# The forward substitution of eight head pairs: VectorE or POOL, in a hybrid decoder step whose order a planner sets

## The chip, the core and the metric

The kernel runs on one core of one Trainium2 chip. Its engines are TensorE (PE; its weight loads are listed as PEld), VectorE (DVE), ScalarE (ACT), GpSimd (POOL) and SyncE (SP, which here issues DMAs). The metric is the device time of one launch in microseconds; lower is better.

## What is computed

One step of a decoder layer, for 512 prompt tokens and 8 sample tokens together (520 columns, in chunks of 260), width 1024: an RMS norm, then two branches on the same normalised input, dilated window attention (three groups of 8 heads) and RWKV-7 time mixing (16 heads of 64), merged by sigmoid gates, an output projection and a SwiGLU FFN. What the change touches is the time mixing, whose reference is a scan over tokens:

```python
def step(S, inp):
    r_t, w_t, k_t, v_t, kk_t, a_t = inp
    sa = jnp.einsum('bhij,bhj->bhi', S, -kk_t)
    S = (S * w_t[:, :, None, :] + sa[..., None] * (kk_t * a_t)[:, :, None, :]
         + v_t[..., None] * k_t[:, :, None, :])
    return S, jnp.einsum('bhij,bhj->bhi', S, r_t)
...
y_a = o_a @ lw['w_proj_a']
y_b = o_b @ lw['w_proj_b']
merged = jax.nn.sigmoid(gate_a) * y_a + jax.nn.sigmoid(gate_b) * y_b
out = merged @ lw['w_out']
```

## The kernel before

**Large products.** Every weight is split into two parts (`whi`, `wlo`) and every activation too (`hh`, `hl`), and each 128x128 block takes three matmuls of 128x260 (written `mm<-hh,whi` and so on). They carry most of the program. ACT makes `whi`, DVE makes `wlo`, from blocks that SP loads.

**Time mixing in chunks.** The 16 heads are 8 pairs, p = 0 to 7, and the 512 prompt tokens are 8 chunks of 64. For each pair there are these steps:

- `pair(p)` prepares the operands: matrices `GH` (two tiles, one for each head), `AR`, `KB`, `VT`, and starts `back(p)`, which is the rest.
- `solve(p)` inverts the diagonal 32x32 blocks of the lower triangular matrices in `GH` by forward substitution. Four DMAs on SP bring the blocks to DRAM (`TD`), four bring the coefficients back with one block a partition (`LT`, 128 partitions). `X` starts as the identity by five memsets. Then come 31 steps of two operations: `xt = X[:, :m, s] * LT[s]` and `X += xt`, with m = s // 4 + 1 and w = 31 - s, so m·w elements a partition (1 to 76; the sum over the steps is 1560). Four DMAs write `X` to DRAM (`TE`), four read it back into `GH`. Transposes on DVE (`T`) and small matmuls (`ax<-T,GH`, `ax<-GH,QI`) finish the 64x64 inverse. `SOLVERS` = 2 solves may be in flight (two buffers each of `LT` and `X`), and every `SOLVE` = 3 steps the code hands over to the planner.
- `turn_a(p)` and the first part of `chain(p)` multiply by the inverse. The sequence of `ax<-T,GH` and what follows up to the first chain step is called the turn here. It needs pair p-1's turn to be past.
- `chain(p)` walks the eight chunks: PE `ch<-VTr,GH` and `ch<-AR`, then ACT writes `GH`, then PE `ch<-GH,KB`, then DVE updates the state in `AR`. The steps of one pair are serial; two pairs' chains can run side by side. After them come the output products (`ch<-GH`, `ch<-AR`, called the y product), a copy, a group norm, and the pair's output `OB`.

**What sets the order.** One build-time planner, `Weave`, writes the whole program. It keeps a model clock for each engine (`Clocks`), in which each operation has a price (`Unit.price`), and takes in turn from a main list of large products and from side generators (`pair`, `back`, the sample tokens) whatever its model says is ready. So the engine on which an operation stands, and its price there, move other engines' instructions. The model's prices of the two engines:

```python
if self.name == "POOL":
    return 0.25 + n / 480
if self.name != "PE":
    return 0.07 + n / 960
```

The main list is: the attention and r, k, v projections; 16 gate jobs (`fill`) and 8 jobs of w_proj_a (`pas`), which fill the space between chains; then w_proj_b, w_out, FFN. The w_proj_a jobs load `ga` on POOL's queue into buffers that share the tag `LT`, multiply on DVE and store to `TAD` on POOL's queue. w_proj_b's output blocks n = 0 and n = 1 are begun with the first 7 of 8 input blocks, which need `OB` of pairs 0 to 6 alone, and closed with the last one.

Every operation is recorded by one helper, so all rows show line L380; rows are told apart by tile names.

Of the kernel before, what the change touches and what calls it, by code (L numbers as in the profile page):

```python
# [12 lines left out]
ALU = mybir.AluOpType  # L13
# [12 lines left out]
NP = HB // 2  # L26
# [195 lines left out]
def _bc(ap, shape):  # L222
    return ap.to_broadcast(shape)
# [242 lines left out]
def program(tc, I, O):  # L466
    nc = tc.nc
    ck = Clocks()
    V, S, G, SY = (Unit(n, e, tc, ck) for n, e in (("DVE", nc.vector), ("ACT", nc.scalar), ("POOL", nc.gpsimd), ("SP", nc.sync)))
# [4 lines left out]
    wv = Weave(ck, tc)  # L474
    uid = [0]

    def nm(s):
        uid[0] += 1
        return f"{s}_{uid[0]}"

    def pool(name, stack, **kw):
        return Pool(stack.enter_context(tc.tile_pool(name=name, bufs=1, reuse_waits="tile", **kw)), ck)
# [13 lines left out]
    def bank():  # L496
        return axp.tile([128, 512], FP, name=nm("ax"), tag="ax", bufs=3)
# [153 lines left out]
    def full(tag, bufs=1, dt=FP):  # L651
        return ep.tile([128, NT], dt, name=nm(tag), tag=tag, bufs=bufs)
# [621 lines left out]

    def solve(p):
        r2, QI, GH = rw["r2"], rw["QI"], rw["GH", p]
        TD = drp.tile([4, NC, 32, 32], FP, name=nm("TD"))
        TE = drp.tile([4, NC, 32, 32], FP, name=nm("TE"))
        for q in range(4):
            b = q % 2  # L1280
            SY.dma_start(out=TD[q].rearrange("c s t -> s c t"), in_=GH[q // 2][q * 32:q * 32 + 32, :, b * 32:b * 32 + 32])
        if p >= SOLVERS:
            yield from wv.until("x", p - SOLVERS)

        LT = r2.tile([128, 31, 32], FP, name=nm("LT"), tag="LT", bufs=SOLVERS)
        Xs = r2.tile([128, 8, 32], FP, name=nm("X"), tag="X", bufs=SOLVERS)
        V.memset(Xs[:], 0.0)
        for a in range(4):
            V.memset(Xs[a * 32:a * 32 + 32].rearrange("p m t -> p (m t)")[:, a:256:36], 1.0)
        yield (TD,)  # L1290
        for a in range(4):
            SY.dma_start(out=LT[a * 32:a * 32 + 32], in_=TD[:, :, :31].rearrange("q c s t -> (q c) s t"))
        yield (LT,)
        for s in range(31):
            m = s // 4 + 1
            w = 31 - s
            t = r2.tile([128, 128], FP, name=nm("xt"), tag="xt")
            tv = t[:, :m * w].rearrange("p (m w) -> p m w", m=m)
            V.tensor_tensor(out=tv, in0=_bc(Xs[:, :m, s:s + 1], [128, m, w]),
                            in1=_bc(LT[:, s:s + 1, s + 1:], [128, m, w]), op=ALU.mult)  # L1300
            V.tensor_tensor(out=Xs[:, :m, s + 1:], in0=Xs[:, :m, s + 1:], in1=tv, op=ALU.add)
            if s % SOLVE == SOLVE - 1:
                yield (Xs,)
        yield (Xs,)
        te = TE[:].rearrange("q c (j b) t -> (q c) j b t", b=4)
        for a in range(4):
            SY.dma_start(out=te[:, :, a], in_=Xs[a * 32:a * 32 + 32])
        wv.set("x", p)
        yield (TE,)
        for q in range(4):  # L1310
            b = q % 2
            SY.dma_start(out=GH[q // 2][q * 32:q * 32 + 32, :, b * 32:b * 32 + 32], in_=TE[q].rearrange("c j t -> j c t"))
        yield GH
        if p:
            yield from wv.until("at", p - 1)
        T1 = r2.tile([128, NC, 32], FP, name=nm("T1"), tag="AT")
        for h in range(2):
            V.transpose(out=T1[H[h]], in_=GH[h][H[h], :, 0:32])
        yield T1, BANK
        ps = bank()  # L1320
        for c in range(NC):
            for h in range(2):
                a, b = (slice(h * 64 + i, h * 64 + i + 32) for i in (0, 32))
                E.matmul(ps[b, c * 32:c * 32 + 32], lhsT=GH[h][a, c, 32:64], rhs=T1[a, c], start=True, stop=True)
        for h in range(2):
            b = slice(h * 64 + 32, h * 64 + 64)
            S.copy(out=QI[b], in_=ps[b, :256].rearrange("p (c x) -> p c x", c=NC))
        yield QI, BANK
        ps = bank()
        for c in range(NC):  # L1330
            for h in range(2):
                a, b = (slice(h * 64 + i, h * 64 + i + 32) for i in (0, 32))
                E.matmul(ps[a, c * 32:c * 32 + 32], lhsT=QI[b, c], rhs=GH[h][b, c, 32:64], start=True, stop=True)
        for h in range(2):
            a = slice(h * 64, h * 64 + 32)
            S.copy(out=GH[h][a, :, 32:64], in_=ps[a, :256].rearrange("p (c x) -> p c x", c=NC))
        wv.set("solved", p)
        yield GH
# [128 lines left out]
    def back(p):  # L1467
        yield from solve(p)
        yield from wv.until("w0", p)
        yield from turn_a(p)  # L1470
        yield from chain(p)
        if p == NP - 3:
            for i in range(NP - 2):
                yield from wv.until("pair", NP - 1)
                t = full("tmp", 2)
                G.dma_start(out=t[:, :T], in_=OBD[:, i])
                yield (t,)
                o = ob_tile(i)
                split(o[:, 0, :T], o[:, 1, :T], t[:, :T])
                wv.set("ob", i)  # L1480
# [208 lines left out]
    def pb_pre(n):  # L1689
        def pre():  # L1690
            if n == 0:
                yield from wv.until("ob", NP - 3)
                hctx.close()
                mp = mrg["pool"] = pool("mg", mctx, side="right")
                mrg["h"] = mp.tile([128, KD, NT], FR, name="mh")
                mrg["l"] = mp.tile([128, KD, NT], FR, name="ml")
            gb = gp_.tile([128, NT], FP, name=nm("gb"), tag="g", bufs=2)
            ta = full("tmp", 2)
            G.dma_start(out=gb[:], in_=GD[:, KD + n])
            G.dma_start(out=ta[:], in_=TAD[:, n])  # L1700
            mrg[n] = gb, ta
            yield ()
        return pre
# [264 lines left out]
```

## Time and profile before

| | us |
|---|---|
| median of 3 runs | 1312.92 (1310.77 to 1315.44) |
| profiled execution | 1316.53 |
| its span, first to last instruction | 1314.8 |
| PE busy | 1264.7 (96%) |
| DVE busy | 843.7 (64%) |
| ACT busy | 610.6 (46%) |
| POOL busy | 175.0 (13%) |
| mean granted TensorE clock | 0.983 |

Of the page, the lines of slices give an engine's busy share in 40 equal parts of the span, here 32.9 us each, in tenths. The groups give busy time and mean duration of instructions with the same tiles. A row of the timeline begins with start and duration in us, and ends with what the engine waited for, if it did. `windows` rows give busy time in a stretch.

### The profile page before, as it was taken

Reading aid. Unit: us, or ns where it says so; the run is one execution under the profiler, and the core shown is the slowest. Engines: PE = TensorE matmul, PEld = TensorE weight load, DVE = VectorE, ACT = ScalarE, POOL = GpSimd, SP = SyncE. Lnnn points to the kernel's source line nnn. Section 1 sums busy time; section 2 is a strip of 40 time slices with the busy share of each in tenths; the row PEclk is TensorE's granted clock in tenths of the full one; section 3 lists DMA queues with packets and bytes.
Section 4 is the critical chain, followed back from the end, with each engine's and each line's share of the span. In section 5 each row is a group of like instructions: output and inputs, shape, how many; then the busy total and the mean of one; then the engine's idle time right before and its main releaser. Section 6 shows DMA issues by size and latency. Waiting matters only on the chain.

```text
span 1314.8 us, 29468 instructions
## 1 busy us (share of the span) xinstructions
PE 1264.7 (96%) x11738; PEld 1197.5 (91%) x11738; DVE 843.7 (64%) x2221; ACT 610.6 (46%) x1554; POOL 175.0 (13%) x261
## 2 busy tenths in 40 slices
PE   7999999999989989999999999999999999999996
PEld 7998999989978878888888888999999999999996
DVE  6956866954869998886986665555843444332333
ACT  5244244366656656675785665334433232222220
POOL 1300100100223332121123122110200000000000
PEclk9999999999989999997999999999999999999998
DMA  6523654634245554543245454552222222223331
GB/s 215 158 94 96 213 178 146 221 112 172 69 131 136 152 147 141 143 156 97 77 139 168 123 175 157 182 192 85 81 97 97 97 89 89 97 93 89 89 101 65
DMA packets 92137, 169.48 MB, mean 129 GB/s; under 512 B 42416, under 2 KB 47568, under 8 KB 92000
## 3 DMA queue, kind: packets, MB, share of 16 engines
q1 hardware_dynamic: 60880, 102.46, 24.6%
q0 software_dynamic: 14512, 46.47, 11.5%
q10 hardware_dynamic: 16608, 18.68, 4.3%
q8 instruction: 92, 1.51, 0.5%
q14 instruction: 45, 0.37, 0.1%
HBM read 133.20 MB, written 27.94 MB: 123 GB/s over the span
## 4 chain that ended last, share of the span: by engine, by line
PE 64%; DVE 15%; issue 9%; DMA 6%; ACT 4%; POOL 1%; SPq 1%; ACTq 0%; DVEq 0%; POOLq 0%
PE mm L380 51%; PE ax L380 8%; PE ch L380 5%; DVE wlo L380 2%; DVE X L380 1%; DVE xt L380 1%; DMA fb<-FD 1%; DMA sw<-raw 1%; ACT KB L380 1%; DVE k L380 1%; DMA raw<-w_in 1%; SPq L380 1%; DVE raw L380 1%; DVE qk L380 1%; DVE GH L380 1%
## 5 line engine op out<-in xcount | busy, mean ns | idle before, releaser
L380 PE MATMUL mm<-hh,whi 128*128 128x260 f32 x1136 | 340.2, 299 | 0.8 <-ACT gt L380 0.8
L380 PE MATMUL mm<-hh,wlo 128*128 128x260 f32 x1136 | 325.4, 286 | 4.3 <-DVE wlo L380 4.3
L380 PE MATMUL mm<-hl,whi 128*128 128x260 f32 x1136 | 325.7, 287 | 0.0
L380 ACT CAST whi<-raw 128x1024 fp32r<-128x1024 f32 (+1 forms) x165 | 170.1, 1032 | 324.4 <-PE mm L380 290.6
L380 DVE TENSOR_TENSOR wlo<-raw,whi 128x1024 fp32r<-128x1024 f32 (+1 forms) x165 | 197.9, 1199 | 140.2 <-ACT whi L380 137.0
L380 PEld LDWEIGHTS mm<-hh,whi 128*128 128x128 f32 x1136 | 215.7, 190 | 13.3 <-issue 6.0
L380 PEld LDWEIGHTS mm<-hh,wlo 128*128 128x128 f32 x1136 | 215.4, 190 | 6.5 <-DVE wlo L380 5.8
L380 PEld LDWEIGHTS mm<-hl,whi 128*128 128x128 f32 x1136 | 215.5, 190 | 1.4 <-issue 0.2
L380 PE MATMUL mm<-h2l,whi 128*128 128x260 f32 x608 | 171.5, 282 | 0.0
L380 PE MATMUL mm<-h2h,wlo 128*128 128x260 f32 x608 | 171.4, 282 | 0.0
L380 PE MATMUL mm<-h2h,whi 128*128 128x260 f32 x608 | 171.4, 282 | 0.0
L380 PEld LDWEIGHTS mm<-h2h,wlo 128*128 128x128 f32 x608 | 114.5, 188 | 0.0
L380 PEld LDWEIGHTS mm<-h2l,whi 128*128 128x128 f32 x608 | 114.4, 188 | 0.0
L380 PEld LDWEIGHTS mm<-h2h,whi 128*128 128x128 f32 x608 | 114.4, 188 | 0.0
L380 PE MATMUL mm<-fh,wlo 128*128 128x260 f32 x388 | 109.6, 282 | 0.0
L380 PE MATMUL mm<-fh,whi 128*128 128x260 f32 x388 | 109.5, 282 | 0.0
L380 PE MATMUL mm<-fl,whi 128*128 128x260 f32 x388 | 109.5, 282 | 0.0
L380 PEld LDWEIGHTS mm<-fh,whi 128*128 128x128 f32 x388 | 73.1, 188 | 0.0
L380 PEld LDWEIGHTS mm<-fl,whi 128*128 128x128 f32 x388 | 73.0, 188 | 0.0
L380 PEld LDWEIGHTS mm<-fh,wlo 128*128 128x128 f32 x388 | 72.9, 188 | 0.0
L380 DVE TENSOR_TENSOR xt<-X,LT 128x60 f32<-128x60 f32 (+24 forms) x248 | 60.3, 243 | 3.6
L380 DVE TENSOR_TENSOR X<-X,xt 128x60 f32<-128x60 f32 (+24 forms) x248 | 57.6, 232 | 3.8
(390 smaller groups left out, 2588.8 us busy)
## 6 DMA issues: line engine op xcount, KB each, us to landing
raw<-w_in SPq DMA_DIRECT2D x77, 512.0 KB, 3.7
raw<-w_gate SPq DMA_DIRECT2D x22, 512.0 KB, 3.2
raw<-w_up SPq DMA_DIRECT2D x22, 512.0 KB, 3.2
raw<-w_down SPq DMA_DIRECT2D x16, 512.0 KB, 3.5
kt<-kcache POOLq DMA_DIRECT2D x24, 256.0 KB, 3.7
kt<-vcache POOLq DMA_DIRECT2D x24, 256.0 KB, 3.5
sw<-raw ACTq DMA_DIRECT2D x64, 65.0 KB, 3.6
GD<-gt ACTq DMA_DIRECT2D x16, 260.0 KB, 3.0
```

What stands on the lines that cost most here:

```text
L380: r = f(*a, **k)
```

## The change

The forward substitution's memsets and its 62 operations a pair are issued on POOL (`G`) instead of DVE (`V`). The main list gains one wait: block n = 1 of w_proj_b may not begin until the last pair's chain has recorded its output copy.

```diff
     def solve(p):
         r2, QI, GH = rw["r2"], rw["QI"], rw["GH", p]
+        B = G
...
-        V.memset(Xs[:], 0.0)
+        B.memset(Xs[:], 0.0)
         for a in range(4):
-            V.memset(Xs[a * 32:a * 32 + 32].rearrange("p m t -> p (m t)")[:, a:256:36], 1.0)
+            B.memset(Xs[a * 32:a * 32 + 32].rearrange("p m t -> p (m t)")[:, a:256:36], 1.0)
...
-            V.tensor_tensor(out=tv, in0=_bc(Xs[:, :m, s:s + 1], [128, m, w]),
+            B.tensor_tensor(out=tv, in0=_bc(Xs[:, :m, s:s + 1], [128, m, w]),
                             in1=_bc(LT[:, s:s + 1, s + 1:], [128, m, w]), op=ALU.mult)
-            V.tensor_tensor(out=Xs[:, :m, s + 1:], in0=Xs[:, :m, s + 1:], in1=tv, op=ALU.add)
+            B.tensor_tensor(out=Xs[:, :m, s + 1:], in0=Xs[:, :m, s + 1:], in1=tv, op=ALU.add)
...
     def pb_pre(n):
...
+            if n == 1:
+
+                yield from wv.until("chain", NP - 1)
```

The order of PE's instructions changes with it, since the planner prices these operations differently. The numbers behind tile names count the tiles as they are made, and are those of one program alone. PE in before, where the chain of pair 4 (`VTr_7889`) runs beside that of pair 5 (`VTr_8320`), with gate work (`mm`) between:

```order
L380 MATMUL ch_10211<-VTr_7889,GH_7440 64x64
L380 MATMUL ch_10211<-VTr_7889,GH_7441 64x64
L380 MATMUL ch_10211<-AR_7327 64x64 x2
L380 MATMUL ch_10218<-VTr_8320,GH_8126 64x64
L380 MATMUL ch_10218<-VTr_8320,GH_8127 64x64
L380 MATMUL ch_10218<-AR_7936 64x64 x2
L380 MATMUL mm_10175<-hh,whi_9889 128x260
L380 MATMUL mm_10175<-hl,whi_9889 128x260
L380 MATMUL mm_10175<-hh,wlo_9890 128x260
L380 MATMUL mm_10175<-hh,whi_9889 128x260
L380 MATMUL mm_10175<-hl,whi_9889 128x260
L380 MATMUL mm_10175<-hh,wlo_9890 128x260
```

PE in after, in the chain of pair 5 (`VTr_8417`):

```order
L380 MATMUL ch_10663<-VTr_8417,GH_8007 64x64
L380 MATMUL ch_10663<-VTr_8417,GH_8008 64x64
L380 MATMUL ch_10663<-AR_7843 64x64 x2
L380 MATMUL ch_10663<-GH_8007,KB_8400 64x64
L380 MATMUL ch_10663<-GH_8008,KB_8400 64x64
L380 MATMUL ch_10705<-VTr_8417,GH_8007 64x64
L380 MATMUL ch_10705<-VTr_8417,GH_8008 64x64
L380 MATMUL ch_10705<-AR_7843 64x64 x2
L380 MATMUL ch_10705<-GH_8007,KB_8400 64x64
L380 MATMUL ch_10705<-GH_8008,KB_8400 64x64
```

In before a chain step is followed by another pair's step and by gate matmuls; in after the same pair's next step follows at once. Over the whole of PE, 3366 matmuls of 128x260 stand ahead of pair 4's turn in before and 3786 in after; from that turn to the last chain's end it is 540 and 258. The total is the same.

POOL in before, at the sample tokens' work for the first pair:

```order
L380 TENSOR_TENSOR st_4602<-st_4602,sg_4289 128x512
L380 TENSOR_TENSOR svd_4865<-uk,sel 48x256
L380 TENSOR_TENSOR svd_4876<-uk,sel 48x256
L380 DMA oo_5097<-OTD 128x512
L380 DMA OAD<-oac_4632 128x512
```

POOL in after, at the same place:

```order
L380 TENSOR_TENSOR st_4602<-st_4602,sg_4289 128x512
L380 TENSOR_TENSOR xt_4805<-X_4617,LT_4616 128x31
L380 TENSOR_TENSOR X_4617<-X_4617,xt_4805 128x31
L380 TENSOR_TENSOR xt_4808<-X_4617,LT_4616 128x30
L380 TENSOR_TENSOR X_4617<-X_4617,xt_4808 128x30
```

Fifty operations of the first solve now stand between the state update (`st`) and the sample tokens' `svd`. At the end of the solves, in after, the operations of the last one stand behind the transfers of w_proj_a:

```order
L380 DMA ga_10770<-GD 128x520
L380 DMA TAD<-ga_10770 128x520
L380 DMA br_11077<-GTD 128x512
L380 DMA ga_10841<-GD 128x520
L380 DMA OBD<-KB_8400 128x512
L380 DMA bvr_11496<-BVD 128x512
L380 DMA TAD<-ga_10841 128x520
L380 TENSOR_TENSOR xt_11079<-X_10211,LT_10210 128x60
L380 TENSOR_TENSOR X_10211<-X_10211,xt_11079 128x6x10
```

So the last solve's operations, and its hold on one of the two `LT` buffers, last until the transfers of w_proj_a ahead of them on POOL's queue have been issued.

## The prediction

> **What bounds the kernel now.** I read the busy times and slices first, then the chain that ended last, then windows cut at the solves and the chains, and last the timeline of single rows.
>
> ```profile
> span 1314.8 us, 29468 instructions
> PE 1264.7 (96%) x11738; PEld 1197.5 (91%) x11738; DVE 843.7 (64%) x2221; ACT 610.6 (46%) x1554; POOL 175.0 (13%) x261
> DVE  6956866954869998886986665555843444332333
> POOL 1300100100223332121123122110200000000000
> PE 64%; DVE 15%; issue 9%; DMA 6%; ACT 4%; POOL 1%; SPq 1%; ACTq 0%; DVEq 0%; POOLq 0%
> ```
>
> PE is busy for 96% of the span: whatever shortens another engine can win only what PE idles, and whatever makes PE idle costs in full. POOL is nearly empty and DVE is full in slices 12 to 16 (361 to 526 us), which speaks for moving work. The next fence has the three stretches in which the eight pairs are solved and chained (the third begins at pair 4's turn and ends at pair 7's y product), and then solve work alone on DVE in the same stretches (us, DVE busy). The columns of the first three rows are us, then busy PE, PEld, DVE, ACT, POOL with counts, then granted clock, DMA share, GB/s.
>
> ```profile
> 365.00:468.00 103.00, 95.02 (x864) 88.10 (x863) 92.13 (x268) 59.22 (x145) 32.19 (x44) 0.97 0.48 134
> 468.00:672.00 204.00, 195.01 (x2189) 171.99 (x2188) 171.58 (x595) 134.90 (x421) 48.22 (x68) 0.95 0.44 130
> 672.10:810.70 138.60, 132.56 (x1694) 116.18 (x1694) 94.39 (x342) 92.86 (x307) 30.13 (x50) 0.99 0.49 152
> ...
> sum 445.60, DVE 120.79; mean DVE 40.26
> ```
>
> Ahead of pair 4's turn PE idles 8.0 + 9.0 = 17.0 us, and the clock's shortfall (3% of 95.0, 5% of 195.0) is another 12.6 us. That 30 us is all that a freer DVE could return there. What PE waited for in 365 to 672 us (us, times, longest):
>
> ```profile
> PE mm L380 <- DVE wlo L380: 3.3, 4, 1.4
> PE ax L380 <- DVE sd L380: 3.2, 1, 3.2
> PE ax L380 <- DVE sg L380: 2.7, 1, 2.7
> PE ch L380 <- DVE AR L380: 1.6, 2, 1.4
> ```
>
> **The moved arithmetic.** A solve is 31 steps of two TENSOR_TENSORs, 62 in all, over 2 x 1560 = 3120 elements per partition (the sum of m·w in the code). On DVE all of them cost 60.3 + 57.6 = 117.9 us, with 40 memsets beside them. POOL never ran this operation on these tiles; its nearest rows are two of its own TENSOR_TENSORs, of 256 and of 512 elements:
>
> ```profile
> L380 DVE TENSOR_TENSOR xt<-X,LT 128x60 f32<-128x60 f32 (+24 forms) x248 | 60.3, 243 | 3.6
> L380 DVE TENSOR_TENSOR X<-X,xt 128x60 f32<-128x60 f32 (+24 forms) x248 | 57.6, 232 | 3.8
> L380 DVE MEMSET X<- x40: 65/65/272, 334.8 to 696.0; 32x8 f32 x32, 128x256 f32 x8
> L380 POOL MEMSET kw<- 128x32 f32 x1 | 0.1, 118 | 0.0
> 621.20 0.61 POOL L380 TENSOR_TENSOR svd<-uk,sel 48x256 f32<-48x256 f32 x1 [10.61 <-ACT uk L380]
> 645.54 1.04 POOL L380 TENSOR_TENSOR st<-st,sg 128x512 f32<-128x512 f32 x1 [8.43 <-PE ax L380]
> ```
>
> The line through the two POOL rows is (1.04 - 0.61)/256 = 1.68 ns an element and 0.18 us fixed. A solve is then 62 x 0.18 + 3120 x 1.68 ns = 16.4 us, 0.26 us an operation against DVE's 0.24. From below the price is POOL's small memset, 0.118 us; from above the whole 0.61 us of the svd row. I take 0.26, because these operations have 1 to 76 elements and so lie below both rows, plus an estimated 0.06 of hand-over (DVE's rows below leave 0.04 between dependent operations): 0.32 us, 20 us a solve, 160 us for eight. The five memsets cost some 5 x 0.118 us a solve and lie beside the load of the coefficients, so nothing. The four stores and loads around a solve stay on SP's queue, now behind POOL's last step instead of DVE's; weight loads queued behind them are two jobs ahead of PE. I take nothing for that, with a bound of 10 us for all (1.3 a pair).
>
> Is POOL then the bound? In the three windows it is busy 32.2 + 48.2 + 30.1 = 110.5 us of 445.6. With 8 x 16.4 = 131 more it has 242. It is not, at this price.
>
> There is a contention to see:
>
> ```profile
> 517.30 0.61 POOL L380 TENSOR_TENSOR svd<-uk,sel 48x256 f32<-48x256 f32 x1 [2.27 <-ACT uk L380]
> 517.33 0.61 DVE L380 TENSOR_TENSOR xt<-X,LT 128x24 f32<-128x24 f32 x1
> 517.98 0.18 DVE L380 TENSOR_TENSOR X<-X,xt 128x24 f32<-128x24 f32 x1
> 518.20 0.18 DVE L380 TENSOR_TENSOR xt<-X,LT 128x16 f32<-128x16 f32 x1
> ```
>
> A DVE row with two operands that starts 0.03 us after a POOL row ends with it, at 0.61 us instead of about 0.18. So POOL's 496 operations can hold up DVE, and DVE's long ones POOL's. The Trainium skill states this ("SBUF — State Buffer", section "Who interferes with whom"): a DVE instruction with two SBUF inputs and a GpSimd instruction that reads SBUF exclude each other, and whoever issues first keeps the shared ports for its whole instruction. The rows agree. If every instruction of the two engines excluded each other, DVE's other work (92.1 + 171.6 + 94.4 - 120.8 = 237 us) and POOL's 242 would need 479 us in turn, where my forecast below gives the same stretch 511: tight, not decisive. So DVE gets back less than its 118 us. Of the waits above, the four rows come to 10.8 us; I take 11 as what PE gains ahead of pair 4's turn, with 0 and 30 as ends.
>
> **The moved order.** This is the larger part. The price of an operation on POOL enters the planner, so PE's program is another one. PE's rows ahead of pair 4's turn hold 420 more fill matmuls (128x260) than before, and correspondingly fewer follow. What one costs, what a turn and a step of the chain cost:
>
> ```profile
> 1000.00:1025.00 25.00, 25.00 (x212) 25.00 (x211) 10.50 (x16) 8.21 (x12) 0.00 (x0) 1.00 0.25 85
> ...
> 672.10 0.69 PE L380 MATMUL ax<-T,GH 32*32 32x32 f32 x32
> ...
> 744.08 0.69 PE L380 MATMUL ax<-T,GH 32*32 32x32 f32 x32
> ...
> 753.41 0.33 PE L380 MATMUL ch<-VTr,GH 64*64 64x64 f32 x4
> ...
> 727.38 0.33 PE L380 MATMUL ch<-VTr,GH 64*64 64x64 f32 x4
> ...
> 729.73 0.33 PE L380 MATMUL ch<-VTr,GH 64*64 64x64 f32 x4
> ...
> 732.75 0.33 PE L380 MATMUL ch<-VTr,GH 64*64 64x64 f32 x4
> ```
>
> A fill matmul is 25.00/212 = 0.118 us. Pair 4's turn, at 672.1, moves by 420 x 0.118 = 49.6 plus about 2 for 29 more small rows, to 723.7, and by the 11 us back to 712.7.
>
> From there on before has 540 fill matmuls in 138.6 us, and its steps carry two chains at once: in the order shown above, pair 4's and pair 5's rows stand in turn, and a step of both takes 2.35 to 3.02 us. After has 258 fill matmuls, and its chains come one behind the other, pair 5's eight steps back to back with nothing between. A step waits for ACT and DVE in turn, so without fill and without a second chain it still takes its latency. I sum the serial tail:
> - three turnovers from a pair's turn to its first chain step, 753.41 - 744.08 = 9.3 us each, and 3 for the first one: 31. Pair 4's turn itself is the start.
> - 24 steps of pairs 5, 6 and 7 alone, between 2.35 and 3.02, at 2.7: 65.
> - 8 steps of pair 4 with 138 fill matmuls (16 us) among them, half of it hidden: 2.7 + 1.0 each: 30.
> - four y products, 1.15 + 0.68 = 1.8 each by the first two rows below: 7.
> - the eight jobs of w_proj_a, 120 fill matmuls: 14.
> - hand-over of ga's buffers, 10. In after the last solve keeps one of the two buffers that the ga loads share. One hand-over is the store's wait and the load's landing, 2.06 + 4.0 us by the last rows below, some 4 us more than a job's 15 matmuls; I take two and a half of them as uncovered.
> - clock: one stretch more like that at 585 us, 33 x (1 - 0.74) = 8.6, so 9.
>
> ```profile
> 809.77 1.15 PE L380 MATMUL ch<-GH 128*64 128x64 f32 x32
> 810.85 0.68 PE L380 MATMUL ch<-AR 64*64 64x64 f32 x14
> ...
> 827.54 0.69 DVE L380 TENSOR_TENSOR OB<-KB,OB 128x512 fp32r<-128x512 f32 x1 [0.69 <-ACT OB L380]
> ...
> 833.87 0.40 PE L380 MATMUL mm<-OB,whi 128*128 128x260 f32 x2
> ...
> 585.00:618.00 33.00, 30.39 (x225) 26.80 (x223) 25.09 (x98) 17.61 (x45) 5.49 (x7) 0.74 0.30 93
> ...
> 773.44 0.54 POOL L380 DMA_DIRECT2D ga<-GD  x1 [2.06 <-DMA TAD<-ga]
> ...
> ga<-GD POOLq DMA_DIRECT2D x8, 260.0 KB, 4.0
> ```
>
> Sum: 31 + 65 + 30 + 7 + 14 + 10 + 9 = 166 us, so the last y product ends at 712.7 + 166 = 878.7 (811.5 in before). After it stands the last group norm. In before its output is ready at 828.2, 16.7 us after the y product, and PE, which had gate work left, reaches its first use at 833.9, 5.7 later. In after the gates are used up and PE has some 70 matmuls (8 us) of w_proj_b, so the norm ends last: 878.7 + 16.7 = 895.4. From the first use of the last pair's output on, both programs hold the same work. The difference is 895.4 - 833.9 = +61.5.
>
> The new wait holds w_proj_b's second output block, in the order in which the program is written, until the last chain's output copy is recorded. It adds no instruction; what it moves is the w_proj_b work behind the last y product, which hides 8 of the 16.7 us of the norm, and so it costs nothing in the sum beside the order that is counted there.
>
> The profiled execution took 1316.5 us, 1.7 more than its span and 3.6 more than the median of the runs shown, 1312.9. 1316.5 + 61.5 = 1378.0; on the median's footing 1374.4.
>
> **The rivals.**
> - Thin tail, as summed. Ends: tail 132 (24 x 2.35 = 56, 8 x 3.0 = 24, turnovers, y and w_proj_a as above, no hand-over, full clock) to 205 (24 x 3.02, 8 x 5.1, 20 of hand-over, 20 of clock). With DVE relief 30 to 0 that is 1321 to 1424, so 1338 to 1410 without both ends at once. Chance 0.70.
> - POOL becomes the bound. The rule of exclusion makes it so, if most of POOL's operations wait for a DVE row of 0.6 us and more. Its eight solves must fit between 384 us and about 875 us beside 110 us of other work: (491 - 110)/496 = 0.77 us an operation decides. My price is 0.32; with half of them waiting 0.3 it is 0.47. At 0.9 us PE loses another 496 x 0.13 = 64 us, so 1400 to 1440. Chance 0.15.
> - Not slower: lone steps are short. If a step without fill takes 2.0 us, because the 2.35 held fill and a second chain, 32 steps are 64; with 31 + 7 + 14 the tail is 116 us. With the full relief of 30 the first use is at 723.7 - 30 + 116 + 16.7 = 826.4, 7 us earlier: 1305. It decides at a tail of 123 us with full relief, 104 with 11. For it speaks DVE's 88% in 365 to 672 us; against it that PE waited there for DVE a mere 11 us. Chance 0.06.
> - The order costs, but less: tail near 130 and some relief, 1321 to 1338. Chance 0.09.
>
> **The numbers.** A measurement of this kernel tells about 0.3% (4 us) from no change. Slower by more: 0.70 + 0.15 + 0.09 less a little, 0.93; within it 0.03; faster 0.04. The time of the likeliest is 1374. The range 1332 to 1416 leaves out the faster rival, most of the last, and about half of POOL's.
>
> **What would show it.** In the profile after: TENSOR_TENSORs of X and xt on POOL at 0.2 to 0.3 us each and DVE's total down by about 118 us; pair 4's turn at 700 to 725 us; lone chain steps 2.35 to 3.0 us apart; the stretch from the turn to the last y product 130 to 200 us long with PE well below its 96%, and idle time put down to ACT GH and DVE AR; the stretch after the first use of the last pair's output unchanged. I am wrong if X operations on POOL show 0.5 us or more and PE waits for solves, if the turn comes before 695, or if steps without fill take 2 us.

## The result, and the profile after

The change makes the kernel slower: a median of 1500.09 us (1497.16 to 1502.12, 4 runs) against 1311.85 us (1308.75 to 1315.44, 4 runs) of before on the same chip, a ratio of 1.1432 with a 95% interval of 1.1396 to 1.1468. The forecast was 1374 with a range of 1332 to 1416: right in direction, but about a third of the loss. The lines of the page of after that answer to those shown of before:

```profile
span 1495.4 us, 29484 instructions
PE 1325.7 (89%) x11738; PEld 1245.5 (83%) x11738; DVE 761.3 (51%) x1685; ACT 611.4 (41%) x1554; POOL 349.4 (23%) x797
PE   7999999999584589788798857878999999999997
DVE  7848859546555245366262524335575434342333
POOL 1201102002766661612615272201100000000000
PEclk9999999999796689987899758658999999999998
PE 41%; POOL 6%; issue 4%; DVE 4%; DMA 3%; ACT 1%; SPq 0%; DVEq 0%; POOLq 0%; ACTq 0%
L380 POOL TENSOR_TENSOR xt<-X,LT 128x54 f32<-128x54 f32 (+24 forms) x248 | 87.7, 354 | 33.6 <-DMA LT<-TD 15.1
L380 POOL TENSOR_TENSOR X<-X,xt 128x54 f32<-128x54 f32 (+24 forms) x248 | 85.7, 345 | 18.6
```

No engine is full. PE fell from 96% to 89% busy, DVE from 64% to 51%, POOL is at 23%, and still the program is 181 us longer in the span. PE is busy 61 us more with the same 11738 matmuls: the granted clock is down in most of slices 11 to 28, the slices in which PE is less busy too. Four rows of PE place the loss: pair 4's turn, the last y product (two rows), and the first use of the last pair's output, which in before stood at 672.1, 811.5 (its end) and 833.9.

```profile
823.54 0.69 PE L380 MATMUL ax<-T,GH 32*32 32x32 f32 x32
...
999.54 0.70 PE L380 MATMUL ch<-GH 128*64 128x64 f32 x8
1000.16 1.50 PE L380 MATMUL ch<-AR 64*64 64x64 f32 x28
...
1013.33 0.59 PE L380 MATMUL mm<-OB,whi 128*128 128x260 f32 x1 [3.81 <-ACT OB L380]
```

Pair 4's turn is 151 us late. From it to the first use of the last output it takes 189.8 us, against 161.8 in before: 28 more. Behind that use the two programs run alike (1495.4 - 1013.3 = 482.1 us to the span's end, 480.9 in before). Five sixths of the loss is thus ahead of pair 4's turn. That stretch as a whole, of after and then of before (us, busy PE, PEld, DVE, ACT, POOL with counts, clock, DMA share, GB/s):

```profile
365.00:823.50 458.50, 365.06 (x3515) 330.59 (x3514) 214.01 (x490) 213.82 (x589) 226.58 (x546) 0.86 0.37 106
```

```profile
365.00:672.10 307.10, 290.12 (x3051) 260.09 (x3050) 263.81 (x862) 194.22 (x566) 80.41 (x111) 0.96 0.45 131
```

PE idles 93 us of it instead of 17, although POOL is busy for less than half. What PE waited for there, and then what DVE waited for (total, times, longest):

```profile
PE ax L380 <- POOL svd L380: 34.2, 5, 10.7
PE ax L380 <- DVE sg L380: 24.6, 4, 20.9
PE ch L380 <- DVE AR L380: 13.3, 1, 13.3
PE ax L380 <- DVE st L380: 10.8, 1, 10.8
```

```profile
DVE AR L380 <- PE ch L380: 57.3, 25, 4.3
DVE oo L380 <- DMA fb<-FD: 54.1, 6, 22.6
DVE st L380 <- PE ax L380: 38.7, 8, 10.8
...
DVE KB L380 <- DMA br<-GTD: 13.3, 1, 13.3
```

The second DVE row is the key. `fb` is a load of the attention merge, which has nothing to do with the solve, but POOL issues it. The timeline of POOL shows where it stands, with the DVE rows and the PE row that follow from it:

```profile
446.05 0.23 POOL L380 TENSOR_TENSOR xt<-X,LT 128x28 f32<-128x28 f32 x1
446.53 0.60 POOL L380 DMA_DIRECT2D oo<-OTD  x1 [0.25 <-issue]
447.15 0.25 POOL L380 TENSOR_TENSOR X<-X,xt 128x28 f32<-128x28 f32 x1
447.33 0.63 POOL L380 DMA_DIRECT2D fb<-FD  x1
...
453.51 0.80 DVE L380 TENSOR_TENSOR oo<-oo,fb 128x512 f32<-128x512 f32 x1 [16.28 <-DMA fb<-FD]
464.50 0.69 DVE L380 TENSOR_TENSOR oo<-oo,fb 128x512 f32<-128x512 f32 x1 [8.72 <-DMA fb<-FD]
465.12 0.16 DVE L380 SCALAR_TENSOR_TENSOR sg<-pv,sd 128x8 f32<-128x8 f32 x1
...
465.42 0.58 PE L380 MATMUL ax<-ident,sg 128*16 128x128 f32 x2 [20.86 <-DVE sg L380]
```

The load was issued behind a run of 41 solve operations (427.7 to 446.1). DVE stood at the product with `fb` for 16.3 and then 8.7 us; `sg`, an operation of 0.16 us for the sample tokens, stood behind it in DVE's order; PE waited 20.9 us for `sg`. Each engine's in-order list passed the delay on to the next. The waits for `svd` are the short form of it. `svd` runs on POOL itself and stood behind 36 solve operations, from 378.5 us on (ahead of the prediction I had put fifty there; the program and the trace both have 36). The last of them, `svd`, and PE:

```profile
396.05 0.32 POOL L380 TENSOR_TENSOR X<-X,xt 128x70 f32<-128x70 f32 x1
396.32 0.60 POOL L380 TENSOR_TENSOR svd<-uk,sel 48x256 f32<-48x256 f32 x1
...
396.98 0.79 PE L380 MATMUL ax<-svd,uk 48*128 48x256 f32 x1 [10.73 <-POOL svd L380]
```

The other two large waits of PE end in the same way. The 10.8 us for `st` lie behind the longest wait of DVE for `fb`, 22.6 us. The 13.3 us for `AR` lie behind DVE's 13.3 us for `br`, a load of the gates that POOL issued at 631.6, right behind its solve operations. Together that is 34.2 + 20.9 + 10.8 + 13.3 = 79 of the 93 us in which PE was idle.

### The profile page after: what moved, and what is told of

Its sections match the earlier page's. It is cut to its first block, busy times and chain, and to the rows that moved or that the text cites. A ratio compares the mean times of both kernels' runs of the same rounds, so it can differ in the third digit from the quotient of the medians.

```text
span 1495.4 us, 29484 instructions
## 1 busy us (share of the span) xinstructions
PE 1325.7 (89%) x11738; PEld 1245.5 (83%) x11738; DVE 761.3 (51%) x1685; ACT 611.4 (41%) x1554; POOL 349.4 (23%) x797
## 4 chain that ended last, share of the span: by engine, by line
PE 41%; POOL 6%; issue 4%; DVE 4%; DMA 3%; ACT 1%; SPq 0%; DVEq 0%; POOLq 0%; ACTq 0%
PE mm L380 34%; PE ax L380 4%; PE ch L380 3%; POOL X L380 3%; POOL xt L380 3%; DMA LT<-TD 1%; DVE KB L380 1%; DMA TAD<-ga 1%; DMA ga<-GD 0%; DVE wlo L380 0%; ACT GH L380 0%; DVE rst L380 0%; DMA kt<-kcache 0%; DMA kt<-vcache 0%; ACT KB L380 0%
## 5 line engine op out<-in xcount | busy, mean ns | idle before, releaser
L380 PE MATMUL mm<-hh,whi 128*128 128x260 f32 x1136 | 345.5, 304 | 0.0
L380 PE MATMUL mm<-hh,wlo 128*128 128x260 f32 x1136 | 331.7, 292 | 3.3 <-DVE wlo L380 3.3
L380 PE MATMUL mm<-hl,whi 128*128 128x260 f32 x1136 | 331.4, 292 | 0.0
L380 PEld LDWEIGHTS mm<-hh,whi 128*128 128x128 f32 x1136 | 221.8, 195 | 12.5 <-issue 6.6
L380 PEld LDWEIGHTS mm<-hh,wlo 128*128 128x128 f32 x1136 | 221.8, 195 | 5.0 <-DVE wlo L380 4.1
L380 PEld LDWEIGHTS mm<-hl,whi 128*128 128x128 f32 x1136 | 221.9, 195 | 1.3
L380 POOL TENSOR_TENSOR xt<-X,LT 128x54 f32<-128x54 f32 (+24 forms) x248 | 87.7, 354 | 33.6 <-DMA LT<-TD 15.1
L380 POOL TENSOR_TENSOR X<-X,xt 128x54 f32<-128x54 f32 (+24 forms) x248 | 85.7, 345 | 18.6
L380 ACT ACTIVATE GH<-ch,DN 64x64 f32<-64x64 f32 x128 | 39.5, 308 | 83.3 <-PE ch L380 81.0
```

The costliest lines, as they stand in the source:

```text
L380: r = f(*a, **k)
```

## The experiments

Two theories. Queue: what is slow is POOL's in-order list, on which foreign work stands behind solve operations. Order: what is slow is PE's program as the planner moved it, as I had forecast. A third, speed, came up on the way: the solve itself takes longer on POOL. Each ratio is against before on the same chip. Whether after would run without the added wait was not tried.

**The wait alone.** Before, with the wait of three lines in `pb_pre`.

```diff
+            if n == 1:
+                yield from wv.until("chain", NP - 1)
```

> Before with the added wait on the last chain alone; PE's order of matmuls is the one of before. Every theory: no change, 1308 to 1317 us. If the wait itself costs, over 1320.

1313.35 us, ratio 1.0004 (0.9982 to 1.0025). The wait costs nothing here.

**The order without the engine.** The solve stays on DVE, through a unit that the planner prices as POOL.

```diff
+    VP = Unit("POOL", nc.vector, tc, ck)
...
-        B = G
+        B = VP
```

> The solve runs on DVE again, but the planner prices it as on POOL, so PE has the order of after (3786 fill matmuls ahead of pair 4's turn, as in after) and no solve operation stands on POOL's queue. Queue theory (what is slow is the in-order queue of POOL: transfers of the attention merge and the sample tokens' products stand behind solve operations, DVE and PE wait for them): 1360 to 1390 us, the price of the order alone, as my forecast had it. Order theory (PE's moved order is the loss): 1490 to 1510 us.

1404.07 us, ratio 1.0688 (1.0652 to 1.0724), 14 us over the top of what the queue theory gave and 96 under after. The order theory as the whole is out, and the order alone costs more than the queue theory allowed it.

**The engine without the order.** The solve on POOL, priced as on DVE.

```diff
+    GD_ = Unit("DVE", nc.gpsimd, tc, ck)
...
-        B = G
+        B = GD_
```

> The solve runs on POOL, but the planner prices it as on DVE, so PE has the order of before (3366 fill matmuls ahead of pair 4's turn), and POOL's queue still has up to 36 and more solve operations ahead of the merge's transfers and the sample products. Queue theory: 1400 to 1500 us. Order theory: 1310 to 1325 us.

1413.13 us, ratio 1.0771 (1.0731 to 1.081). Neither theory is the whole: the order alone costs about 91 us, the engine alone 100, and together, in after, 188. Their turns of pair 4, first the order alone and then the engine alone:

```profile
744.41 0.69 PE L380 MATMUL ax<-T,GH 32*32 32x32 f32 x32
```

```profile
746.07 0.69 PE L380 MATMUL ax<-T,GH 32*32 32x32 f32 x32
```

72 and 74 us late, and 151 in after: here too the two add up. With the engine alone the waits of before's order are those of after's, PE's first and then DVE's, from 365 to 746 us:

```profile
PE ax L380 <- POOL svd L380: 27.7, 5, 10.7
PE ax L380 <- DVE GH L380: 21.2, 5, 13.1
PE ax L380 <- DVE sg L380: 7.2, 2, 4.1
```

```profile
DVE oo L380 <- DMA fb<-FD: 38.8, 6, 16.4
DVE st L380 <- PE ax L380: 29.9, 7, 10.9
DVE oac L380 <- DMA fb<-FD: 21.6, 2, 15.9
```

**POOL's queue cleared.** After, with the sample products on DVE and the transfers that POOL issues from the chains to w_proj_b on SP (`oo` and `fb` stand for them). The loads of the caches (`kt`, 16 of them) and 24 operations on `GH` and `AR` stay on POOL.

```diff
-                G.dma_start(out=oo[:], in_=OTD[:, hp, g])
+                SY.dma_start(out=oo[:], in_=OTD[:, hp, g])
...
-                    G.dma_start(out=fb[H[h2]], in_=FD[:, h, g].unsqueeze(0).to_broadcast([64, 4, 128]))
+                    SY.dma_start(out=fb[H[h2]], in_=FD[:, h, g].unsqueeze(0).to_broadcast([64, 4, 128]))
...
-        G.tensor_tensor(out=st[:], in0=st[:], in1=_bc(g[:, G_W].unsqueeze(2), [128, NS, 64]), op=ALU.mult)
+        V.tensor_tensor(out=st[:], in0=st[:], in1=_bc(g[:, G_W].unsqueeze(2), [128, NS, 64]), op=ALU.mult)
...
-            G.tensor_tensor(out=t[:], in0=_bc(uk[:, 0].unsqueeze(1), [48, 4, 64]),
+            V.tensor_tensor(out=t[:], in0=_bc(uk[:, 0].unsqueeze(1), [48, 4, 64]),
```

> After with POOL's queue cleared: the transfers that POOL issued from the first chain on, those of the merge among them, go to SP, and the sample tokens' two kinds of products to DVE; the solves stay on POOL. Queue theory: the waits of DVE for the merge's transfers (54 us) and of PE for the products (34 us) go, 1340 to 1400 us. Speed theory (a solve on POOL is simply too long, 26 to 29 us, for the pairs' sequence): stays over 1450 us.

1356.67 us, ratio 1.0323 (1.0284 to 1.0363): 143 of the 188 us are gone with the solve still on POOL. The order changed too: 3215 fill matmuls now stand ahead of pair 4's turn, not 3786. The planner's model has an in-order POOL as well; with the queue cleared it no longer expects the chains late, and doesn't push fill ahead of them. That suggests that much of the price of the order was the same congestion, as the planner foresaw it; no run shows it apart.

**Each half of the clearing.** The merge's loads alone to SP (the first two changes of the diff above), and the sample products alone to DVE (the last two).

> After, with the 36 loads of the attention merge (oo and fb) issued on SP instead of POOL; the planner moves fill with it (3504 ahead of pair 4's turn, 3786 in after). Queue theory: DVE's 62 us of waits for fb and PE's for sg and st behind it go, PE's 34 us for svd stay: 1420 to 1460 us. If the products on POOL alone hold PE up: 1490 to 1505 us.

1407.35 us, ratio 1.0719 (1.0685 to 1.0753): 93 us of after's loss, more than the 40 to 80 that I gave it.

> After, with the sample tokens' products (svd, 16) and state scaling (st, 8) on DVE; the merge's loads stay on POOL. Queue theory: PE's 34 us for svd go, DVE's waits for fb stay: 1450 to 1480 us. If the merge's loads are all of it: 1490 to 1505 us.

1452.16 us, ratio 1.1046 (1.1003 to 1.1088): 48 us, as expected. Both halves hold, and 93 + 48 = 141 is nearly the 143 of both. The planner moved fill in each of them (3504 and 3619 matmuls ahead of pair 4's turn, not 3786), so neither number is the queue alone.

**The cleared queue in before's order, and its control.** The run above with the solve priced as on DVE; and before, solve on DVE, with the same clearing. The edits are those of the two diffs above together, and the second alone.

> The solve on POOL, priced as on DVE, with POOL's queue cleared as in the run of that kind before (transfers on SP, sample products on DVE): PE's order is close to that of before (3348 fill matmuls ahead of pair 4's turn). If order and queue are the whole loss: 1305 to 1325 us, and a chance of below before, since DVE is rid of 118 us. Speed theory (POOL's longer solves themselves): 1340 to 1360 us.

> Control: before, solve on DVE, with the same transfers on SP and the same sample products on DVE. If the clearing itself is neutral: 1308 to 1325 us. Against it the run with the solve on POOL in nearly the same order shows what the engine alone does: queue theory at most 10 us between them, speed theory 25 or more.

The first took 1365.98 us, ratio 1.0402 (1.0364 to 1.044), more than any of my cases; the second 1300.91 us, ratio 0.9902 (0.9865 to 0.9938), 7 us below the range of a neutral clearing. Their PE orders are almost the same (3348 fill matmuls ahead of pair 4's turn in both), and 65 us lie between them, where the queue theory gave at most 10. The turns of pair 4, solve on POOL and then on DVE:

```profile
709.12 0.69 PE L380 MATMUL ax<-T,GH 32*32 32x32 f32 x32
```

```profile
649.72 0.69 PE L380 MATMUL ax<-T,GH 32*32 32x32 f32 x32
```

It does not follow that the 65 us are the speed of the solve alone, since its queue was not free of other work and the transfers went to a list that waits for the solve too. What DVE waited for with the solve on POOL, from 350 to 900 us, and a piece of SP's list:

```profile
DVE oo L380 <- DMA fb<-FD: 31.0, 3, 15.3
DVE kt L380 <- DMA kt<-kcache: 26.9, 5, 11.4
```

```profile
417.32 0.33 SPq L380 DMA_DIRECT2D lwr<-w_lora  x1
432.81 0.60 SPq L380 DMA_DIRECT2D TE<-X  x1
433.51 0.55 SPq L380 DMA_DIRECT2D oo<-OTD  x1
434.15 1.26 SPq L380 DMA_DIRECT2D fb<-FD  x2
```

SP stood for 15.2 us ahead of `TE`, the solve's own store, until POOL had done its step, and the merge's next loads were issued behind it; DVE waited 14.1 us for them. `kt` is still issued on POOL, between solve operations. In the control DVE waited 0.2 us for `fb` and 2.8 for `kcache` in the same two places. PE's largest wait, 19.3 us in three, was for `st<-swkv`, another load that had been moved to SP. So the bound of 10 us is missed, but a slower solve and the lists behind it are not parted by this pair.

**Half a solve.** The first of these two with every second step of a solve left out, counted in the plan all the same.

```diff
+            xin, lin = _bc(Xs[:, :m, s:s + 1], [128, m, w]), _bc(LT[:, s:s + 1, s + 1:], [128, m, w])
+            if s % 2 == 0:
+                B.tensor_tensor(out=tv, in0=xin, in1=lin, op=ALU.mult)
+                B.tensor_tensor(out=Xs[:, :m, s + 1:], in0=Xs[:, :m, s + 1:], in1=tv, op=ALU.add)
+            else:
+                xo = Xs[:, :m, s + 1:]
+                ck.run("DVE", [tv], [xin, lin], B.price("tt", [tv], [xin, lin]))
+                ck.run("DVE", [xo], [xo, tv], B.price("tt", [xo], [xo, tv]))
```

> The cleared run with the solve on POOL in before's order (1366 us), with every second step of each solve left out: 32 operations a solve instead of 62, while the planner still counts all of them, so PE's order is the same. If the time of a solve on POOL is what that run loses against its control on DVE (1301 us): 1300 to 1325 us. If something else goes with POOL (its hand-overs, the transfers behind it on SP): over 1345 us.

1323.3 us, ratio 1.0067 (1.0042 to 1.0092): inside the first case: 43 of the 65 us go with half of the operations. The loss between the pair hangs on how long a solve takes on POOL. Whether through its own time or through the lists that it holds up, this run can't tell either: with half the operations DVE's waits for `kcache` fall from 26.9 to 13.2 us as well. The remaining 22 us still have half a solve in them and aren't split further.

**What made the control faster.** Before with the transfers alone on SP, as in the clearing.

> Before with the transfers alone moved from POOL to SP, sample products left on POOL; solve on DVE. If the transfers' place makes the control faster than before: 1298 to 1305 us. If it is the products on DVE: 1310 to 1318 us.

1311.72 us, ratio 0.999 (0.9963 to 1.0016). My first case is refuted: the transfers' place is not what wins 1%. It needs the sample products on DVE; whether these alone do it was not run. The control is 1% faster than before, and the fastest version here: one that takes work off POOL, and gives it to DVE.

**Four pairs at a time.** The last four on POOL, and then, in a second run, the first four:

```diff
-        B = G
+        B = G if p >= 4 else V
```

```diff
-        B = G
+        B = G if p < 4 else V
```

> After with only pairs 4 to 7 solved on POOL, pairs 0 to 3 on DVE. The merge's transfers then stand ahead of all solve operations (as in before), the sample products of pairs 4 to 7 behind some. Queue theory: most of the loss is with the merge, so 1340 to 1390 us. If each pair costs alike: 1400 to 1410 us.

1373.98 us, ratio 1.0447 (1.0393 to 1.0502).

> After with only pairs 0 to 3 on POOL, pairs 4 to 7 on DVE: POOL's queue is that of after up to the merge's end. Queue theory: 1430 to 1480 us. If each pair costs alike: 1400 to 1410 us.

1424.48 us, ratio 1.0832 (1.077 to 1.0895), a little under the queue theory's range. The first four pairs, whose solves overlap the merge, cost 110 us over before, the last four 59. Pairs do not cost alike. That it is the merge that makes the difference is likely but not shown, since the planner moved fill as well (3660 matmuls ahead of pair 4's turn with the first four pairs on POOL, 3270 with the last four).

## Why the prediction was wrong, point by point

**What bounds the kernel.** Right: PE idle time and clock are the currency. What I drew from it was half: I counted what a freer DVE could return (0 to 30 us) and not what a busier POOL could take.

**Price of an operation.** 0.26 us was nearly right for POOL alone, and too low beside DVE. Two stretches of the solve in after, the first with DVE busy, the second with DVE idle, then single rows of the second and of the first, with the DVE row that the last but one ran into (columns of the first two: us, busy PE, PEld, DVE, ACT, POOL):

```profile
427.60:437.40 9.80, 8.96 (x75) 8.46 (x76) 9.60 (x20) 3.64 (x8) 8.54 (x18) 1.00 0.32 85
437.40:446.10 8.70, 7.16 (x90) 6.74 (x88) 0.00 (x0) 8.07 (x22) 6.82 (x25) 1.00 0.09 32
```

```profile
438.04 0.29 POOL L380 TENSOR_TENSOR xt<-X,LT 128x54 f32<-128x54 f32 x1
438.41 0.29 POOL L380 TENSOR_TENSOR X<-X,xt 128x54 f32<-128x54 f32 x1
...
429.14 1.21 DVE L380 TENSOR_TENSOR wlo<-raw,whi 128x1024 fp32r<-128x1024 f32 x1
429.25 1.20 POOL L380 TENSOR_TENSOR xt<-X,LT 128x29 f32<-128x29 f32 x1
430.53 0.29 POOL L380 TENSOR_TENSOR X<-X,xt 128x29 f32<-128x29 f32 x1
```

With DVE idle the 23 operations that lie wholly in the second stretch take 0.29 us each (the count of 25 has two more that it cuts) and follow each other every 0.36 (forecast 0.26 and 0.32). With DVE busy one took 1.20 us with 29 elements, four times its neighbour: it began 0.11 us behind a DVE subtraction of two operands and ended 0.10 us behind it. Over all 496 the mean is (87.7 + 85.7)/496 = 0.35 us; the 327 that overlap no DVE instruction average 0.28, the other 169 0.48. So the exclusion that the prediction took from the Trainium skill ("SBUF — State Buffer", "Who interferes with whom") shows in the other direction too: here the one that came second was POOL's, and it waited. That is 0.20 us more for each of the 169, 34 us in all. I had noted it as a loss of DVE's gain and, outside the rival with POOL as the bound, not as a price of the solve.

**The step that failed: what pair 4's turn gains.** The prediction put the turn at 723.7 by the moved order and took "the 11 us back", to 712.7. Measured is 823.5, 100 us later than the first. The order alone gave 744.4: 21 of it. In that run PE was busy for 65 us more than in before, where I had 51.6, at a granted clock of 0.94 instead of 0.96, and idle for 24 us instead of 17. The stretch with the order alone:

```profile
365.00:744.40 379.40, 355.09 (x3521) 321.88 (x3519) 288.81 (x917) 214.73 (x591) 79.18 (x114) 0.94 0.45 129
```

The other 79 come with the solve on POOL, in the same PE order: foreign work behind solves on POOL's queue, and the longer solve, which makes that work later still. The sum had no term for either. I took the place of POOL's DMAs for the last solve only, where the order was quoted, and let the merge's 36 loads and the sample products pass, though the order quoted ahead of the prediction shows solve operations between `st` and `svd`. A sum of busy time (242 of 446 us) cannot see that; POOL was never full. None of the signs that I had named for being wrong came: X took 0.35 us and not 0.5, the turn was late and not early, and lone steps took 2.34 us and not 2. Among the signs of being right, "pair 4's turn at 700 to 725 us" failed.

**The transfers behind the solve on SP.** Nothing, with a bound of 10 us, held in after: PE waited 1.5 us for weights ahead of pair 4's turn. In the cleared runs the same list also carried the merge's loads, and held them up (above).

**The relief from DVE.** DVE's busy time fell by 82 us net, but PE gained nothing that shows: DVE now waited for loads that POOL had not issued. (It was busy for 86% of 365 to 672 us in before, not the 88% of the prediction, and full from slice 13 on, not 12.)

**The moved order and the serial tail.** The mechanism held, and the sum came out close, in part by luck. From pair 4's turn to the end of the last y product I summed 166 us; after took 178.1 and the run with the order alone 164.9. The last norm took 11.7 us in both, where I had 16.7. But the terms were not those of the sum. The 258 matmuls of that stretch were 192 of w_proj_a (24 a job; I had 120, 15 a job), 6 of the gates (I had 138) and some 60 of w_proj_b. Lone steps took 2.34 us (pair 6's start at 955.08, 957.42 and 959.76) where I had 2.7, and the waits for `ga` were 13.3 us where I had 10. And the clock fell over the whole stretch, to 0.66, where I had one more piece of 33 us:

```profile
823.50:1000.20 176.70, 133.09 (x1376) 108.52 (x1372) 66.94 (x194) 79.81 (x293) 59.04 (x145) 0.66 0.30 89
```

**The added wait.** Nothing, as forecast, in before's order.

**The rivals.** POOL as the bound had 0.15 and was put at 1400 to 1440, decided at 0.77 us an operation. It did not decide so: 0.35 us was enough, since order on the queue and not throughput held PE up. The right place had the wrong mechanism. The faster rival is out: lone steps took 2.34 us and not 2.0, and no relief of DVE reached PE.

## What to carry to other kernels

Before moving work to an idle engine, list what else that engine issues, DMAs above all, and who waits for each: its busy share says nothing about what will stand behind the new work. In a program that a planner writes, price the move twice, once for the order that the planner makes of it and once for the engine; here the two were about equal and added up. Taking the unrelated loads and products off the queue recovered three quarters of the loss, and on the kernel before, the same clearing gained 1%. But look at the list to which they go: SP's waits for the same solve.

## What the runs showed of the hardware

On POOL a TENSOR_TENSOR of 54 elements a partition took 0.29 us with DVE idle, and one of 29 elements took 1.20 us when it began behind a DVE subtraction of 1.21. In before it was the other way round: a DVE operation of 24 elements took 0.61 us beside a POOL row of 0.61.

The granted clock of PE was lower where PE had gaps. In after it was 0.66 over 177 us in which PE was busy for 75%, and 0.86 over the 458 us ahead of them at 80%; in before it was 0.96 over 307 us at 94%. Over the whole program PE was busy 61 us longer with the same 11738 matmuls. What sets the clock was not tested.
